# Order of VectorE's work at the end of the head and in the first group of a Strassen-like matmul with RMS norm

## The chip, the cores and the metric

The kernel runs on one core of one Trainium2 chip. The metric is the time of one execution on the device in microseconds (us), lower is better. The time before is the median of three runs.

## The reference

```python
def reference(a, b, gamma, eps):            # all 2048 x 2048, fp32
    x = np.matmul(a, b)
    rms = np.sqrt(np.mean(x ** 2, axis=-1, keepdims=True) + eps)
    return (gamma * x / rms).astype(np.float32)
```

A row of the output needs the whole row of the product (for the root mean square of its 2048 values) before it can be scaled.

## The kernel before

**Tiling.** A is cut into 16 row blocks of 128 rows. B lies in SBUF as bf16, in two halves of 1024 columns (half 0 and half 1), each as two chunks of 512. The first four blocks (0 to 3, `HB = 4`) are the *head*: they are computed while B still arrives. Blocks 4 to 15 follow in six *groups* of two blocks, numbered 2 to 7 (`G0 = 2`), and each group in two halves.

**A group's half** (`group_half`, L576) computes a 256 x 1024 piece of the output by a scheme of Strassen's kind: seven *products* of eight matmuls of 128x512 in place of eight products. Product 1 uses the sum of two quarters of A, product 2 another, and so on; the sums of A (`a_sums`, L254, recorded as L260) are made by VectorE into the five tiles `s_1, s_2, s_5, s_6, s_7`, the sums of B lie ready. The order on TensorE is 2, 5, 1, 4, 3, 7, 6 (5 before 2 in the very first half). Products 4 and 3 add onto the banks of products 2 and 5 (`start=False`), so those banks must have been read before: by ScalarE's copy at L591 and by VectorE's addition at L595. The other evictions are L599 (VectorE, product 1), L602 (ScalarE, product 4's bank), L604 (VectorE, SBUF alone), L607 (ScalarE, product 3's bank), L609 (VectorE, SBUF alone), L613 and L618 (VectorE, products 7 and 6). PSUM has seven banks in the pool `acc` and one more, `tbank`; a new product takes the bank that has been free longest.

**The head's end.** The right half of blocks 2 and 3 (`r2`, `r3`; the code calls them rows) is also made by the seven products; their banks are `pair[2], pair[5], pair[1], p7, p6`. The additions that end these rows stand in three places: the subtraction that reads `pair[1]` (L551), `pair_sums` (L561, L562, SBUF alone) and `pair_ends` (L565, L566, which read `p7` and `p6`). Around L551 stand A's sum 5 for group 2, the copies of block 5's transposes (`take_transposed`, L192), the squares of rows 0 and 1 on ScalarE (`square_half`, L310), `take_rms(0)` (a reduce on VectorE, L335, and a square root on ScalarE, L337), and A's sums 2 and 1.

**Next rows.** While a group is computed, the next two blocks of A are prepared: `row_norm` (ScalarE: two squares L219 and a root L222), `row_factor` (VectorE: four one-column operations, L227 to L232, which bring the block into range for fp16), and `row_apply` (ScalarE: one 128x2048 scaling into fp16, L242), after which the SP queue issues a DMA transpose (L195). `finish(row, halves)` scales rows that are complete (VectorE, `scale`, L370) and stores them (SP queue, L376). POOL's queue loads blocks of A (L116, L121); before some of the loads POOL waits by a one-column copy (L127).

**What sets the order.** The order on each engine is the order in which the program text issues instructions (`tc.manual_schedule()`); waits between engines are derived from the tiles. Work from outside a group is put between its products by *hooks*: `hook(n, f, ...)` in `hooks_of` (L628) appends `f` to a list that `group_half` runs at its n-th place (`at_hook(n)`). Hook 0 stands ahead of the first product, hook 1 behind the first and its copy L591, hook 2 behind the second and L595, hook 3 behind product 1 and L599, hook 4 behind L604. `last_squares` issues squares that were left from the half before.

Of the kernel before, what the change touches and what calls it, by code (L numbers as in the profile page):

```python
# [13 lines left out]
ALU = mybir.AluOpType  # L14
# [3 lines left out]
def kernel(  # L18
# [13 lines left out]
    nc = tc.nc  # L32
# [12 lines left out]
    G0 = HB // 2  # L45
# [148 lines left out]
    def transpose_dma(mb):  # L194
        nc.sync.dma_start_transpose(at(mb), a16[mb])  # L195
# [40 lines left out]
    def row_apply(mb):  # L236
        a16[mb] = a16_slot(mb)
        if mb < HB + 2:

            nc.vector.tensor_scalar_mul(out=a16[mb], in0=a32.pop(mb), scalar1=factor.pop(mb))  # L240
        else:
            nc.scalar.activation(out=a16[mb], in_=a32.pop(mb), func=ACTF.Copy,  # L242
                                 scale=factor.pop(mb))


    def quarter(g, r, c):
        if g < G0:
            return head_at[:, c::2, 2 * g + r, :]
        return at(2 * g + r)[:, c::2, :]

    def sum_of(g, s):
        return s_sum[s].bitcast(BF16) if g < G0 else s_sum[s]

    def a_sums(g, which, lo=0, hi=KP):  # L254
        a11, a12, a21, a22 = (quarter(g, r, c) for r in range(2) for c in range(2))
        terms = {1: (a11, a22, ALU.add), 2: (a21, a22, ALU.add), 5: (a11, a12, ALU.add),
                 6: (a21, a11, ALU.subtract), 7: (a12, a22, ALU.subtract)}
        for s in which:
            x, y, op = terms[s]
            nc.vector.tensor_tensor(out=sum_of(g, s)[:, lo:hi, :], in0=x[:, lo:hi, :],  # L260
                                    in1=y[:, lo:hi, :], op=op)
# [44 lines left out]
    def square_half(mb, h):  # L306
        c = n_sq[mb]
        n_sq[mb] += 1
        sq = sq_pool.tile([P, 2 * CH], BF16, name="sq")
        nc.scalar.activation(out=sq, in_=x_tile(mb, h), func=ACTF.Square,  # L310
                             scale=inv_sqrt_n, accum_out=msq[mb][:, c:c + 1])

    def x_tile(mb, h):


        if (mb, h) not in x_half:
            n = n_x[0]
            n_x[0] += 1
            if n < 8:
                slot = n  # L320
            else:
                g = n // 4
                slot = ((0, 4, 1, 5), (0, 1, 4, 5))[g // 2 % 2 == 0][n % 4] + 2 * (g % 2)
            x_half[mb, h] = x_slot[slot]
        return x_half[mb, h]

    def x_chunk(mb, c):
        return x_tile(mb, c // 2)[:, (c % 2) * CH:(c % 2 + 1) * CH]
# [3 lines left out]
    def take_rms(mb):  # L332

        tot = stat_pool.tile([P, 1], FP32, name="tot")
        nc.vector.reduce_sum(out=tot, in_=msq.pop(mb), axis=mybir.AxisListType.X)  # L335
        rms_of[mb] = stat_pool.tile([P, 1], FP32, name="rms")
        nc.scalar.activation(out=rms_of[mb], in_=tot, func=ACTF.Sqrt)  # L337
# [123 lines left out]
    pair = {}  # L461
# [57 lines left out]
    x11, x12, x21, x22 = (x_chunk(r, c) for r in (r2, r3) for c in (2, 3))  # L519
# [28 lines left out]
    p6 = new_bank()  # L548
    product(PAIR, 1, 6, p6)
    a_sums(G0, (5,))  # L550
    nc.vector.tensor_tensor(out=x22, in0=pair[1], in1=x22, op=ALU.subtract)  # L551
    for g in range(2):
        turn(HB + 1, g)
        take_transposed(HB + 1, g, turned[HB + 1, g], nc.vector.tensor_copy)
    square_half(0, 1)
    square_half(1, 1)
    take_rms(0)
    a_sums(G0, (2, 1))

    def pair_sums():  # L560
        nc.vector.tensor_tensor(out=x11, in0=x22, in1=x21, op=ALU.add)  # L561
# [66 lines left out]
    def hooks_of(g, j):  # L628


        hooks = {n: [] for n in range(8)}
        nxt = 2 * g + 2

        def hook(n, work, *args):
            hooks[n].append(lambda: work(*args))

        def apply(mb):
            row_apply(mb)
            transpose_dma(mb)

        more = g + 1 < NG
        if j == 0:
            if g == G0:
                hook(0, finish, 0, (1,))
                hook(1, row_norm, nxt)
                hook(1, take_rms, 1)
                hook(2, row_factor, nxt)
                hook(2, finish, 0, (0,))
                hook(2, apply, nxt)
                hook(2, row_norm, nxt + 1)  # L650
                hook(2, a_sums, g, (7, 6))
                hook(2, finish, 1, (1, 0))
                hook(2, row_factor, nxt + 1)
                hook(2, pair_sums)
                hook(2, pair_ends)
                hook(4, apply, nxt + 1)
                hook(7, square_half, r2, 1)
            else:
                done = [2 * g - 2, 2 * g - 1]
                if g == G0 + 1:  # L660
                    done.insert(0, r3)
                else:
                    hook(1, row_norm, nxt)
                for mb in done:
                    hook(1, take_rms, mb)
                hook(2, row_factor, nxt)
                hook(2, apply, nxt)
                if g == G0 + 1:
                    hook(2, finish, r3)
                hook(2, row_norm, nxt + 1)  # L670
                hook(3, scale, 2 * g - 2)
                hook(3, row_factor, nxt + 1)
                hook(4, apply, nxt + 1)
                hook(4, store, 2 * g - 2)
        else:
            if g == G0:
                hook(1, take_rms, r2)
                hook(1, square_half, r3, 1)
                hook(2, finish, r2, (1, 0))
            else:  # L680
                hook(2, finish, 2 * g - 1)
            if more:
                hook(3, a_sums, g + 1, (2, 5, 1))
                hook(6, a_sums, g + 1, (7,))
                hook(7, a_sums, g + 1, (6,))
            if g + 2 < NG:
                hook(0, load_after, g, nxt + 2)
                if g == G0:
                    hook(2, wait_for, x_slot[HB + r2][:, 0:1])
                    hook(2, load_block, nxt + 3)  # L690
                    hook(5, row_norm, nxt + 2)
                else:
                    hook(0, load_block, nxt + 3)
        return hooks
# [113 lines left out]
    for g in range(G0, NG - 1):  # L808
        for j in range(2):
            group_half(g, j, hooks_of(g, j))  # L810
# [35 lines left out]
```

## Time and profile before

| what | us |
|---|---|
| median of three runs | 221.8 (221.38 to 221.89) |
| the profiled execution's own time | 221.69 |
| its span, first to last instruction | 219.9 |
| TensorE busy | 209.3 (95%) |
| VectorE busy | 165.9 (75%) |
| ScalarE busy | 127.0 (58%) |
| mean granted TensorE clock | 0.992 |

The span is 1.8 us shorter than the execution's own time. PE is TensorE's matmuls, PEld its weight loads, DVE VectorE, ACT ScalarE, POOL GpSimd, and SP the sync engine, which here only issues DMAs. In the chain of work that ended last, matmuls of L285 (all products) hold 64% of the span: from 69.3 us on they stand one behind the other to the end. The head takes the 69 us ahead of that, bound at first by the arrival of A and B. In the lines shown below a tile's name has its number left out, so that `x`, `s` and `acc` each stand for several buffers, and a line of the code can be that of a helper.

### The profile page before, as it was taken

The page shows a single profiled execution, that of the slowest core. Times are in us where ns is not written, and L with a number is a line of the kernel's source. Part 1 is how long each engine was busy: PE and PEld are TensorE (multiplying, and loading weights), DVE is VectorE, ACT ScalarE, POOL GpSimd, SP SyncE. Part 2 cuts the span into 40 slices and gives each one's busy share as a digit, 9 for nine tenths or more (in the row PEclk, how much of TensorE's full clock was granted, in tenths as well). Part 3 has the DMA queues.
Part 4 walks back from the last instruction along what each step waited for, and adds up shares of the span by engine and source line. Part 5 has one row for each costly group of instructions (what it writes and reads, how often), then busy time and mean ns, then how long its engine had stood idle before and what let it go on. Part 6 is the DMA issues. An engine that isn't in the chain of part 4 may idle for free.

```text
span 219.9 us, 3044 instructions
## 1 busy us (share of the span) xinstructions
PE 209.3 (95%) x1032; PEld 97.4 (44%) x1032; DVE 165.9 (75%) x326; ACT 127.0 (58%) x263; POOL 36.3 (16%) x75
## 2 busy tenths in 40 slices
PE   7799999999999999999999999999999999999970
PEld 3344544444454444444444444444444444444440
DVE  1128799999889999979795639946695659787781
ACT  2110002920599898688745997289747996334471
POOL 7544443343020002100200002000200000000040
PEclk9999999999999999999999999999999999999996
DMA  7999999999929895948799049965699249145045
GB/s 157 164 203 206 199 206 208 212 206 228 409 76 362 291 293 118 358 176 230 213 300 405 3 93 265 351 247 95 156 294 405 42 100 364 73 174 210 1 171 212
DMA packets 36864, 46.60 MB, mean 212 GB/s; under 512 B 22256, under 2 KB 26352, under 8 KB 35568
## 3 DMA queue, kind: packets, MB, share of 16 engines
q0 software_dynamic: 10608, 23.86, 44.1%
q1 hardware_dynamic: 25824, 22.02, 33.5%
q10 hardware_dynamic: 416, 0.52, 0.7%
q8 instruction: 8, 0.13, 0.2%
q14 instruction: 8, 0.07, 0.1%
HBM read 34.60 MB, written 16.78 MB: 234 GB/s over the span
## 4 chain that ended last, share of the span: by engine, by line
PE 65%; DMA 23%; ACT 4%; POOL 2%; issue 1%; DVE 1%; ACTq 0%; POOLq 0%
PE acc L285 64%; DMA b<-in_b_dram 14%; DMA early<-in_a_dram 5%; DMA a<-in_a_dram 4%; ACT sq L219 2%; POOL b L102 1%; ACT at_even L192 1%; PE acc L790 1%; POOL early L106 1%; DVE s L260 1%; DVE at_even L192 0%; ACT x L729 0%; DVE x L551 0%; ACT norm L222 0%; ACT x L531 0%
## 5 line engine op out<-in xcount | busy, mean ns | idle before, releaser
L285 PE MATMUL acc<-b,s 128*128 128x512 bf16 x408 | 93.3, 379 | 0.5 <-DVE s L260 0.5
L285 PEld LDWEIGHTS <-s 128*128 128x128 f16 (+1 forms) x512 | 49.9, 98 | 60.4 <-DVE s L260 1.0
L388 PE MATMUL acc<-b,head_at 128*128 128x512 bf16 x176 | 43.2, 379 | 1.2 <-DMA b<-in_b_dram 1.2
L303 ACT ACTIVATE sq<-x 128x512 bf16<-128x512 f32 x53 | 33.4, 630 | 6.9 <-DVE x L722 3.0
L370 DVE SCALAR_TENSOR_TENSOR x<-x,r,gamma_sb 128x1024 f32<-128x1024 f32 x28 | 34.8, 1282 | 0.7
L219 ACT ACTIVATE sq<-a 128x1024 bf16<-128x1024 f32 x24 | 25.3, 1053 | 2.1 <-DMA a<-in_a_dram 1.5
L388 PEld LDWEIGHTS <-head_at 128*128 128x128 bf16 x176 | 16.9, 98 | 20.6 <-issue 1.6
L242 ACT ACTIVATE head_at<-a,s 128x2048 f16<-128x2048 f32 x10 | 20.0, 1998 | 3.3 <-DVE s L229 3.3
L102 POOL DMA_DIRECT2D b<-in_b_dram x32 | 17.2, 540 | 20.8 <-DMA b<-in_b_dram 15.0
L430 ACT COPY x<-acc 128x512 f32<-128x512 f32 x5 | 2.9, 582 | 24.7 <-PE acc L388 24.7
L285 PEld LDWEIGHTS <-head_at 128*128 128x128 f16 (+1 forms) x112 | 10.9, 98 | 13.2
L285 PE MATMUL acc<-early,head_at 128*128 128x512 bf16 x64 | 14.5, 379 | 0.0
L285 PEld LDWEIGHTS <-at_even 128*128 128x128 f16 x96 | 9.4, 98 | 11.3
L285 PE MATMUL acc<-early,s 128*128 128x512 bf16 x56 | 14.2, 379 | 0.0
L260 DVE TENSOR_TENSOR s<-head_at 128x1024 f16<-128x1024 f16 (+5 forms) x22 | 13.4, 635 | 0.1
L609 DVE TENSOR_TENSOR x<-x,x 128x512 f32<-128x512 f32 x9 | 6.2, 692 | 8.8 <-ACT x L607 8.3
L127 POOL COPY pace<-x 128x1 f32<-128x1 f32 x4 | 1.7, 413 | 66.7 <-DVE x L618 65.6
L591 ACT COPY x<-acc 128x512 f32<-128x512 f32 x9 | 5.2, 573 | 11.5 <-PE acc L285 11.5
L173 DVE COPY head_at<-tbank 128x1024 bf16<-128x1024 bf16 x7 | 4.8, 692 | 8.7 <-PE tbank L168 8.5
L285 PE MATMUL acc<-t_left,s 128*128 128x512 bf16 x48 | 11.3, 379 | 0.0
L774 POOL TENSOR_SCALAR x<-x,r 128x512 f32<-128x512 f32 x1 | 2.7, 2652 | 51.2 <-DVE r L346 51.2
L276 DVE TENSOR_TENSOR b<-b 128x1024 bf16<-128x1024 bf16 x16 | 10.8, 684 | 0.2
(113 smaller groups left out, 237.5 us busy)
## 6 DMA issues: line engine op xcount, KB each, us to landing
out_dram<-x SPq DMA_DIRECT2D x29, 512.0 KB, 3.8
a<-in_a_dram POOLq DMA_DIRECT2D x10, 1024.0 KB, 8.7
b<-in_b_dram POOLq DMA_DIRECT2D x32, 256.0 KB, 10.0
a<-in_a_dram POOLq DMA_DIRECT2D x4, 512.0 KB, 9.8
early<-in_a_dram POOLq DMA_DIRECT2D x7, 256.0 KB, 10.2
gamma_sb<-in_gamma_dram POOLq DMA_DIRECT2D x2, 512.0 KB, 8.3
out_dram<-x SPq DMA_DIRECT2D x3, 256.0 KB, 2.6
out_dram<-a SPq DMA_DIRECT2D x1, 512.0 KB, 3.3
```

The lines of the kernel that those rows point to most:

```text
L102: nc.gpsimd.dma_start(out=raw[j][kp][:, t, :], in_=b[lo:lo + P, j * HALF:(j + 1) * HALF])
L173: nc.vector.tensor_copy(out=head_at[:, 2 * kp:2 * kp + 2, :, :], in_=view)
L219: nc.scalar.activation(out=junk, in_=a32[mb][:, h * HALF:(h + 1) * HALF], func=ACTF.Square, scale=2.0 ** -8, accum_out=n2[:, h:h + 1])
L242: nc.scalar.activation(out=a16[mb], in_=a32.pop(mb), func=ACTF.Copy, scale=factor.pop(mb))
L260: nc.vector.tensor_tensor(out=sum_of(g, s)[:, lo:hi, :], in0=x[:, lo:hi, :], in1=y[:, lo:hi, :], op=op)
L276: nc.vector.tensor_tensor(out=flat[:, 1:3, :], in0=flat[:, 1:3, :], in1=flat[:, 0::3, :], op=ALU.add)
L285: nc.tensor.matmul(bank, lhsT[:, kp, :], rhs, start=(start and kp == 0), stop=(kp == KP - 1), skip_group_check=not start)
L303: nc.scalar.activation(out=sq[:, 0:CH], in_=src, func=ACTF.Square, scale=inv_sqrt_n, accum_out=msq[mb][:, c:c + 1])
L370: nc.vector.scalar_tensor_tensor(out=x, in0=x, scalar=inverse_of[mb], in1=gamma_sb[:, h * HALF:(h + 1) * HALF], op0=ALU.mult, op1=ALU.mult)
L388: nc.tensor.matmul(bank, head_at[:, kt, r, :], head_rhs(c, kt), start=(kt == 0), stop=(kt == KT - 1))
L591: nc.scalar.copy(out=c, in_=one[1])
L609: nc.vector.tensor_tensor(out=t, in0=t, in1=x12, op=ALU.add)
```

## The change

At the head's end A's sums 2 and 1 for group 2 go ahead of `take_rms(0)`, and the subtraction L551 moves from ahead of the two copies of transposes to behind these sums (and ahead of `take_rms(0)`). In the first half of group 2, in hook 2, `pair_sums`, `pair_ends` and A's sums 7 and 6 go to the front of the list: ahead of the first `row_factor`, of the scalings of rows 0 and 1 and of the second `row_factor`. No instruction is added or taken out.

```diff
     a_sums(G0, (5,))
-    nc.vector.tensor_tensor(out=x22, in0=pair[1], in1=x22, op=ALU.subtract)
     for g in range(2):
         turn(HB + 1, g)
         take_transposed(HB + 1, g, turned[HB + 1, g], nc.vector.tensor_copy)
     square_half(0, 1)
     square_half(1, 1)
+    a_sums(G0, (2, 1))
+    nc.vector.tensor_tensor(out=x22, in0=pair[1], in1=x22, op=ALU.subtract)
     take_rms(0)
-    a_sums(G0, (2, 1))
...
                 hook(0, finish, 0, (1,))
                 hook(1, row_norm, nxt)
                 hook(1, take_rms, 1)
+                hook(2, pair_sums)
+                hook(2, pair_ends)
+                hook(2, a_sums, g, (7, 6))
                 hook(2, row_factor, nxt)
                 hook(2, finish, 0, (0,))
                 hook(2, apply, nxt)
                 hook(2, row_norm, nxt + 1)
-                hook(2, a_sums, g, (7, 6))
                 hook(2, finish, 1, (1, 0))
                 hook(2, row_factor, nxt + 1)
-                hook(2, pair_sums)
-                hook(2, pair_ends)
                 hook(4, apply, nxt + 1)
                 hook(7, square_half, r2, 1)
```

In the two built programs the order of instructions changes on VectorE alone; TensorE, ScalarE, POOL and SP have theirs unchanged. Because banks come free in another order, some products sit in other banks: product 7 and 6 of group 2's half 0 take those of block 5's transposes and of `pair[1]`, and in half 1 products 2 and 5 take the banks of `p7` and `p6`, and product 1 the one that L602 reads.

## The prediction, made before the changed kernel was run

> **What bounds the kernel now.** I read the page first, then TensorE's waits, then the timelines of TensorE, VectorE and ScalarE (columns: start us, length us, engine, line, operation, tiles, count, idle before and its releaser) between 66 and 88 us, where the moved instructions stand.
>
> ```profile
> PE 209.3 (95%) x1032; PEld 97.4 (44%) x1032; DVE 165.9 (75%) x326; ACT 127.0 (58%) x263; POOL 36.3 (16%) x75
> ```
>
> ```profile
> PE acc L147 <- DVE pace L137: 1.4, 1, 1.4
> ...
> PE acc L285 <- DVE s L260: 0.5, 1, 0.5
> ```
>
> TensorE is busy for 95% of the span. In the stretch that the change touches it waits once, for A's sums (L260). All else must show as a TensorE wait or it costs nothing.
>
> ```profile
> 66.97 1.89 PE L285 MATMUL acc<-b,s 128*128 128x512 bf16 x8
> 69.32 1.90 PE L285 MATMUL acc<-b,s 128*128 128x512 bf16 x8 [0.46 <-DVE s L260]
> 71.06 1.89 PE L285 MATMUL acc<-t_left,s 128*128 128x512 bf16 x8
> 72.78 3.62 PE L285 MATMUL acc<-t_left,at_even 128*128 128x512 bf16 x16
> 83.14 1.89 PE L285 MATMUL acc<-early,s 128*128 128x512 bf16 x8
> 84.87 3.62 PE L285 MATMUL acc<-early,at_even 128*128 128x512 bf16 x16
> ```
>
> These are, for group 2 (rows 4 and 5): products 5, 2, 1, then 4 and 3 of half 0; then 1, and 4 and 3, of half 1 (7, 6 and the next 2, 5 lie between). A product takes 1.725 us from start to start (72.78 less 71.06), one matmul 0.216.
>
> ```profile
> 66.66 0.68 DVE L551 TENSOR_TENSOR x<-acc,x 128x512 f32<-128x512 f32 x1
> 68.57 1.29 DVE L260 TENSOR_TENSOR s<-at_even 128x1024 f16<-128x1024 f16 x2
> 71.33 0.69 DVE L595 TENSOR_TENSOR t_first<-acc,head_at 128x512 f32<-128x512 f32 x1
> 72.07 0.15 DVE L227 TENSOR_SCALAR s<-norm 128x1 f32<-128x1 f32 x1
> 78.46 0.68 DVE L561 TENSOR_TENSOR x<-x 128x512 f32<-128x512 f32 x1
> 79.17 0.69 DVE L562 TENSOR_TENSOR x<-x,x 128x512 f32<-128x512 f32 x1
> ```
>
> VectorE has hardly a gap here. Its steps from start to start: 0.60 for a 128x512 or 128x1024 operation, 0.71 where it waits for the result just before it (L561 to L562), 0.70 for the four small row factors, 1.20 for a scaling (L370).
>
> ```profile
> 72.64 2.00 ACT L242 ACTIVATE head_at<-a,s 128x2048 f16<-128x2048 f32 x1 [0.52 <-DVE s L229]
> 77.10 0.57 ACT L602 COPY x<-acc 128x512 f32<-128x512 f32 x1
> 78.33 2.00 ACT L242 ACTIVATE head_at<-a,s 128x2048 f16<-128x2048 f32 x1
> 82.64 0.57 ACT L591 COPY x<-acc 128x512 f32<-128x512 f32 x1
> ```
>
> The reader is to see that ScalarE starts L242 as soon as VectorE's row factor (L229) is there, and then works 10.00 us without a gap until L591 of half 1. That copy ends at 83.21; product 4 of half 1, which adds into the bank that L591 reads, starts at 84.87. The slack is 1.66 us.
>
> **What the Trainium skill says.** PSUM — Partial Sum Buffer, section "Engine vs sequencer instructions": the queues of ScalarE and VectorE are "strict FIFO". The trace agrees: L602's product ended at about 74.7 (72.78 + 1.73 + 0.16), yet it ran at 77.10, behind a normalization that it has nothing to do with. TensorE: Matmul & The Clock Gate, section "Why this matters for your kernels", warns of TensorE gaps over about 3 us, which halve its clock. In this trace the clock is 1.00 for the 3.4 us after the last matmul and 0.51 after that.
>
> **The change, part by part.**
>
> *Head: sums ahead of the subtraction.* VectorE does L260 (sum 5) at 66.05 in both. Then, in place of L551, comes the first L192 copy. It needs the transposes that end at 66.68, so 66.72; the second 67.32; sum 2, which waits for it, 67.32 + 0.71 = 68.03, to 68.72. TensorE was let go 0.06 after the sum before (69.26 to 69.32), so product 2 starts at 68.78; its own order allows 68.48 + 0.22 = 68.70. Gain at this point 0.54. Sum 1 runs at 68.63, its product at 70.51: no wait.
>
> *What the subtraction and take_rms pay.* Subtraction at 69.23, reduce (L335) 69.83 to 69.97 in place of 68.46. Behind that reduce stands ScalarE: the square root (L337) starts 0.04 later, 70.01 to 70.21, and L591 (half 0), queued behind it, ends at 70.74 and not 69.48. VectorE's reciprocal waits for the root: 70.25; scaling 70.44; the next reduce 71.64; L595 at 71.80 to 72.49, against 72.02 before. Product 4 of half 0 adds into the bank that L595 reads: allowed at 70.51 + 1.73 = 72.24, released at 72.49 + 0.06 = 72.55. So 0.31 of the 0.54 is given back; it starts 0.23 ahead of before (72.78).
>
> *First group: six operations ahead of the row factor.* After L595: L561 72.40, L562 73.11, L565 73.72, L566 74.32, sums 7 and 6 at 74.93 and 75.53 (the second ends at 76.21), then L227 at 76.13. Products 7 and 6 start at 76.00 and 77.73 and need the sums by then: done at 75.61 and 76.21, cover 0.39 and 1.5. The banks of pair products 7 and 6 come free near 74.4 and 75.0, some 6 us sooner than before; no matmul waited for them, so nothing is gained.
>
> The factor (L229) is ready at 76.13 + 0.38 + 0.15 = 76.66, and L242 starts at 76.70: 4.06 us later than before (the six operations 3.73, L595's lateness 0.47, less 0.14 for which L227 waited before). ScalarE has idled for it since 73.5. All that is queued behind it moves by as much: the second norm, L602 (ends 81.73), the second L242 (82.39), L607 (ends 84.86), a square, L591 of half 1: 86.70 to 87.27. The second row factor is no tighter: its norm ends at 81.25, VectorE has finished the scalings of rows 0 and 1 by 80.7, the factor is there at 81.8.
>
> TensorE: product 4 of half 0 at 72.55, then 3, 7, 6, 2, 5, 1 at steps of 1.725; product 4 of half 1 could go at 72.55 + 7 x 1.725 = 84.63. It is released at 87.27 + 0.06 = 87.33: a stall of 2.70. Product 1 of half 1 takes the bank that L602 frees (81.73 against 82.90), cover 1.2. Against before: 87.33 - 84.87 = **+2.46 us**, since every later product of before is back to back.
>
> *Moved DMAs.* Of the moved scalings and applies, SP's queue issues, in order: store of x_4 (+0.5), of x_0 (+4.1), the first transpose (near 78.7, its issue takes 3.2), stores of x_5 and x_1 (82.0), the second transpose (84.4, landing 4.6 later, 89.0). L591 of half 1 writes x_5, so it also needs that store landed: 82.0 + 2.9 (as before) = 84.9, against 86.70; the window's slowest store took 6.6, which would give 88.6, 1.9 more stall. POOL waits for the second transpose, so the load of block 8 moves from 85.53 to 89.6 and lands 5.6 later, as before; ScalarE's norm of it and L591 of group 3 follow at 97.9 to 98.4. Group 3's product 2 starts at 84.87 + 6.9 + 2.46 = 94.23, its product 4 needs that copy at 99.41: cover 0.9, used if the load takes over 6.5. Its half 1 is closer: L591 ends at 107.20 + 4.06 = 111.26, product 4 is due at 109.04 + 2.46 = 111.50: cover 0.2. Later ScalarE gaps of 2.1 and 3.8 us, where it waits for TensorE, absorb the rest.
>
> Sum: profiled span 219.9, with 1.8 around it 221.69; 221.69 + 2.46 = 224.15. The median shown is 221.8, 0.1 over that run: **224.2**.
>
> **Unknown costs.** TensorE's release by L595 and L591 isn't seen as a wait in this stretch; I take 0.06 (from L260), bounds 0.0 and 0.2. VectorE's first copy may wait on transposes up to 0.2 longer or not at all: -0.1 to +0.2, since it shifts the whole chain. The store of x_5: nothing to +1.9. Group 3's covers: nothing to +0.8. None can bring a gain beyond 0.2, as each is a wait.
>
> **Rivals.** *Cover holds (not slower).* The end depends on one place, product 4 of half 1. If ScalarE were ready for L591 there by 84.63 - 0.06 - 0.57 = 84.0, so that L242 began by 74.0 (a delay under 1.4 us, not 4.06), nothing would stall and the head's gain stays: 221.69 - 0.23 = 221.5; 221.15 if L595 doesn't stall either. For it: before has 1.66 us of slack, and the change removes the one wait named. Against: ten microseconds of ScalarE work without a gap, in order.
>
> *More behind it.* The same stall, and a second: TensorE is idle from 84.80 (last matmul's end) to 87.33, 2.5 us; a store or load that lands late can stretch it past the 3.4 us at which this trace's clock fell. A restart at 0.51 for about as long (3.4 us) costs 1.7: 225.9. A late x_5 store gives up to 226.1, group 3's covers up to 225.0. Against: 2.5 is under 3.4.
>
> *Less.* VectorE's order is what is built, so the row factor can't come before 75.9; only short waits differ: 223.3.
>
> **How the numbers follow.** Forecast (223.6 to 224.9) 0.64; more behind it (225 to 227) 0.18; less (222.7 to 223.5) 0.06; cover holds (220.9 to 221.6) 0.12. The range 222.9 to 225.9 leaves out the cover case and a few hundredths of the long ones. A measurement of this kernel can tell about 0.3% (0.7 us) from no change: faster (under 221.1) 0.03, same 0.09, slower 0.88.
>
> **What would show it.** Right: L242's idle before the first apply near 3 us behind L229; in TensorE's waits a new line of about 2.7 us, released by ScalarE's L591, near 84.6; one of 0.3 behind L595; L260's 0.5 shrunk to 0.1. Wrong: no TensorE gap near 84 to 88; L242 starting before 74; a gap much over 2.7, or a second one near 99 or 111, or a clock under 1.00 after it.

## The result, and the profile after

The changed kernel takes 227.4 us (median of five, 226.9 to 228.1), 1.025 times the kernel before (95% interval 1.021 to 1.030), whose median in five executions was 221.6; a second set of the changed kernel (227.0, `f0_after_again`, below) gave 1.024 (1.021 to 1.027). It was forecast slower, at 224.2 in a range of 222.9 to 225.9. The direction held, the size did not: about +5.5 us against the +2.4 forecast. The profiled execution took 227.87, with a span of 226.1.

TensorE's waits (the engine and line waited for, then us in total, times, longest), and its timeline from group 2 on:

```profile
PE acc L285 <- ACT x L591: 2.5, 1, 2.5
...
PE acc L285 <- DVE s L227: 0.3, 1, 0.3
```

```profile
73.19 3.61 PE L285 MATMUL acc<-t_left,at_even 128*128 128x512 bf16 x16
...
87.95 5.30 PE L285 MATMUL acc<-early,at_even 128*128 128x512 bf16 x16 [2.52 <-ACT x L591]
...
101.92 1.89 PE L285 MATMUL acc<-t_left,head_at 128*128 128x512 bf16 x8
104.10 1.89 PE L285 MATMUL acc<-t_left,head_at 128*128 128x512 bf16 x8 [0.30 <-DVE s L227]
...
114.76 3.61 PE L285 MATMUL acc<-early,head_at 128*128 128x512 bf16 x15
```

The wait for A's sums (L260) is gone and the forecast stall behind L591 is there (87.95). But the two products that follow it last 5.30 us in place of 3.62, and three more waits stand in group 3, at 101.92, 104.10 and 114.76. (Two of them show only in the start: 1.73 us is a product's step, and these stand 1.93 and 2.03 behind the start before them. For the one at 104.10 the profile names L227; L595, one instruction ahead of it on VectorE and the reader of that bank, ended at 104.05.)

ScalarE, POOL, VectorE and SP in the same stretch:

```profile
70.75 0.20 ACT L337 ACTIVATE rms<-tot 128x1 f32<-128x1 f32 x1 [1.26 <-DVE tot L335]
...
77.34 2.00 ACT L242 ACTIVATE head_at<-a,s 128x2048 f16<-128x2048 f32 x1 [3.27 <-DVE s L229]
...
87.33 0.57 ACT L591 COPY x<-acc 128x512 f32<-128x512 f32 x1
...
98.74 1.06 ACT L219 ACTIVATE sq<-a 128x1024 bf16<-128x1024 f32 x1 [4.11 <-DMA a<-in_a_dram]
...
101.30 0.57 ACT L591 COPY x<-acc 128x512 f32<-128x512 f32 x1
...
114.15 0.57 ACT L591 COPY x<-acc 128x512 f32<-128x512 f32 x1
```

```profile
89.75 1.18 POOL L127 CAST pace<-head_at 128x1 f32<-128x1 f16 x1 [22.68 <-DMA head_at<-head_at]
90.88 0.53 POOL L121 DMA_DIRECT2D a<-in_a_dram  x1
```

```profile
89.60 2.48 DVE L370 SCALAR_TENSOR_TENSOR x<-x,r,gamma_sb 128x1024 f32<-128x1024 f32 x2
90.91 1.53 SPq L376 DMA_DIRECT2D out_dram<-x  x2
```

Before, the same two POOL lines, the stores of row 2 on SP's queue, and the later places that hang on the load read:

```profile
85.02 0.18 POOL L127 CAST pace<-head_at 128x1 f32<-128x1 f16 x1 [18.71 <-DMA head_at<-head_at]
85.53 0.53 POOL L121 DMA_DIRECT2D a<-in_a_dram  x1 [0.32 <-ACT rms L337]
87.05 1.53 SPq L376 DMA_DIRECT2D out_dram<-x  x2
91.24 1.06 ACT L219 ACTIVATE sq<-a 128x1024 bf16<-128x1024 f32 x1 [1.37 <-DMA a<-in_a_dram]
106.64 0.56 ACT L591 COPY x<-acc 128x512 f32<-128x512 f32 x1
109.04 3.62 PE L285 MATMUL acc<-early,head_at 128*128 128x512 bf16 x16
```

The new line to read is L219 at 98.74: ScalarE stands 4.11 us for block 8 of A, then runs to L591 of group 3's half 0 and on to that of half 1, and TensorE waits for both.

The head's end differs by more than 1 us from one profiled execution to the next, of one kernel too. So I count from the first matmul of group 2's product 5 (66.97 before, 67.68 after, 66.54 in the changed kernel's second trace, called "again"):

| start, from product 5's (us) | before | after | again |
|---|---|---|---|
| group 2, half 0, product 4 | 5.81 | -0.30 | -0.30 |
| group 2, half 1, product 4 | 17.90 | +2.37 | +2.36 |
| group 2, half 1, product 7 | 21.35 | +4.06 | +2.36 |
| group 3, half 0, product 4 | 29.99 | +4.25 | +4.32 |
| group 3, half 0, product 3 | 31.72 | +4.70 | +4.77 |
| group 3, half 1, product 4 | 42.07 | +5.01 | +5.06 |
| group 4, half 0, product 1 | 52.43 | +5.01 | +5.06 |

Behind the last row nothing more is lost up to the last product: L790 stands +5.00 in "after". What whole executions show beyond these 5 us lies ahead of product 5 or behind the last matmul.

The two traces of one kernel differ in the middle and agree at the end. In "after" the granted clock fell behind the stall (columns: window; length; busy of PE, PEld, DVE, ACT, POOL; clock, DMA share, GB/s), in "again" it did not:

```profile
88.00:93.00 5.00, 5.00 (x16) 1.94 (x16) 4.19 (x6) 3.74 (x10) 2.85 (x4) 0.66 0.52 133
```

```profile
87.00:92.00 5.00, 5.00 (x25) 2.27 (x24) 4.19 (x6) 4.69 (x13) 2.88 (x4) 1.00 0.51 132
```

The whole executions agree. Of the eleven of the changed kernel, the seven with a mean clock of 0.981 to 0.984 took 227.2 us on average, the three with 0.992 to 0.995 took 227.0 (the eleventh, at 0.988, took 228.1). In "again" the 1.7 us that the clock left alone were waited for in group 3:

```profile
86.80 3.61 PE L285 MATMUL acc<-early,at_even 128*128 128x512 bf16 x16 [2.50 <-ACT x L591]
...
100.85 1.89 PE L285 MATMUL acc<-t_left,head_at 128*128 128x512 bf16 x8 [1.80 <-ACT x L591]
```

So something other than the stall sets the end. The theory: the late work of group 2 delays the load of block 8 (issued 4.6 later than before, landed 6.8 later, both from product 5), and group 3, with 1.78 us to spare for it (in before, product 4 of half 1 starts at 109.04, L591 ends at 107.20, and a release takes 0.06), waits for the rest: 6.80 - 1.78 = 5.02 us, which is what the table shows. Stall and clock lie beneath that wait. The rivals: the stall and the clock's drop simply add up; or other things that moved (banks, the subtraction) cost the time.

### The profile page after: what moved, and what is told of

Its sections match the earlier page's. It is cut to its first block, busy times and chain, and to the rows that moved or that the text cites. A ratio compares the mean times of both kernels' runs of the same rounds, so it can differ in the third digit from the quotient of the medians.

```text
span 226.1 us, 3023 instructions
## 1 busy us (share of the span) xinstructions
PE 211.4 (94%) x1012; PEld 98.4 (44%) x1032; DVE 166.1 (73%) x326; ACT 127.0 (56%) x263; POOL 37.0 (16%) x75
## 4 chain that ended last, share of the span: by engine, by line
PE 50%; DMA 29%; issue 13%; ACT 4%; DVE 1%; POOL 1%; POOLq 0%; ACTq 0%
PE acc L285 49%; DMA b<-in_b_dram 16%; DMA a<-in_a_dram 8%; DMA early<-in_a_dram 4%; ACT sq L219 2%; PE acc L790 1%; ACT sq L303 1%; DVE gamma_sb L240 1%; POOL pace L127 0%; POOL a L121 0%; ACT x L591 0%; ACT x L729 0%; DVE x L595 0%; ACT x L607 0%; POOL gamma_sb L511 0%
## 5 line engine op out<-in xcount | busy, mean ns | idle before, releaser
L388 PE MATMUL acc<-b,head_at 128*128 128x512 bf16 x171 | 42.0, 379 | 1.4 <-DMA b<-in_b_dram 1.3
L370 DVE SCALAR_TENSOR_TENSOR x<-x,r,gamma_sb 128x1024 f32<-128x1024 f32 x28 | 34.8, 1281 | 0.7
L219 ACT ACTIVATE sq<-a 128x1024 bf16<-128x1024 f32 x24 | 25.3, 1054 | 5.0 <-DMA a<-in_a_dram 4.4
L242 ACT ACTIVATE head_at<-a,s 128x2048 f16<-128x2048 f32 x10 | 20.0, 1997 | 6.1 <-DVE s L229 6.1
L285 PE MATMUL acc<-early,at_even 128*128 128x512 bf16 x47 | 12.5, 422 | 2.6 <-ACT x L591 2.5
L260 DVE TENSOR_TENSOR s<-head_at 128x1024 f16<-128x1024 f16 (+5 forms) x22 | 13.4, 635 | 0.1
L127 POOL COPY pace<-x 128x1 f32<-128x1 f32 x4 | 1.3, 320 | 67.4 <-DVE x L618 67.4
L591 ACT COPY x<-acc 128x512 f32<-128x512 f32 x9 | 5.2, 573 | 11.5 <-PE acc L285 7.7
L285 PE MATMUL acc<-t_left,head_at 128*128 128x512 bf16 x48 | 11.0, 379 | 0.3 <-DVE s L227 0.3
```

Of the source, the lines that this page charges most:

```text
L219: nc.scalar.activation(out=junk, in_=a32[mb][:, h * HALF:(h + 1) * HALF], func=ACTF.Square, scale=2.0 ** -8, accum_out=n2[:, h:h + 1])
L285: nc.tensor.matmul(bank, lhsT[:, kp, :], rhs, start=(start and kp == 0), stop=(kp == KP - 1), skip_group_check=not start)
L370: nc.vector.scalar_tensor_tensor(out=x, in0=x, scalar=inverse_of[mb], in1=gamma_sb[:, h * HALF:(h + 1) * HALF], op0=ALU.mult, op1=ALU.mult)
L388: nc.tensor.matmul(bank, head_at[:, kt, r, :], head_rhs(c, kt), start=(kt == 0), stop=(kt == KT - 1))
L591: nc.scalar.copy(out=c, in_=one[1])
```

## The experiments

**The head alone.** `e1_head_only` is the kernel before with the head's half of the diff.

```diff
     a_sums(G0, (5,))
-    nc.vector.tensor_tensor(out=x22, in0=pair[1], in1=x22, op=ALU.subtract)
...
+    a_sums(G0, (2, 1))
+    nc.vector.tensor_tensor(out=x22, in0=pair[1], in1=x22, op=ALU.subtract)
     take_rms(0)
-    a_sums(G0, (2, 1))
```

> Only the head's part of the change. VectorE's row factor comes 0.5 us later than before, so ScalarE's first apply L242 is late by 0.5, inside the 1.66 us of slack ahead of group 2's product 4 of half 1. All theories in which the late row factor is the cause: 0.2 to 0.5 us faster than before (0.54 won at product 2, about 0.3 given back behind L595), 221.0 to 221.4. Rival 'other banks or the subtraction's place is the cause': slower by 1 us or more.

Measured: 222.1 us, 1.0027 (1.0018 to 1.0036): slower, not faster. In its trace the head gain is there (product 4 of half 0 starts 0.31 sooner, from product 5), and it is lost again, with 0.34 more, at one place:

```profile
81.52 1.89 PE L285 MATMUL acc<-b,s 128*128 128x512 bf16 x8 [0.46 <-DVE x L565]
```

Product 5 of half 1 takes the bank of pair product 7, and L565, still at its old place in the queue and now 1.2 us later from product 5 (80.78 less 66.73, against 79.78 less 66.97), frees it too late. In the full change L565 comes early, and its trace has no such wait. So the head's half with its banks costs 0.3%, and the rival's "1 us or more" fails.

**The hooks alone.** `e2_hooks_only` is the changed kernel with the head's half undone.

> Only the first group's part. L242 is late by 3.6 us. 'Stall alone' (the forecast's step): L591 of half 1 lets product 4 go at 86.86 instead of 84.87, +2.0, 223.5; with a clock drop on top ('stall plus clock') +3.7, 225.2. 'Late load' (the late transpose delays the load of block 8 by 3.6 and POOL's wait and the landing add about 2.7; group 3 has 1.8 us of slack for it): +4.6, 226.2, with a TensorE gap at group 3's product 4 of half 1 behind ScalarE's L591.

Measured: 226.3 us, 1.0225 (1.020 to 1.025), 4.8 us more than before by the medians: the "late load" figure, and too much for the stall with or without the clock. The trace shows both waits:

```profile
86.93 3.61 PE L285 MATMUL acc<-early,at_even 128*128 128x512 bf16 x16 [1.79 <-ACT x L591]
...
101.14 5.30 PE L285 MATMUL acc<-t_left,head_at 128*128 128x512 bf16 x16 [1.96 <-ACT x L591]
```

Block 8 landed 30.85 us from product 5, 6.7 later than before. In this execution, which took 227.7, the clock fell behind the second wait, where nothing later hides it; in the other four (226.0 to 226.6) the mean clock was 0.989 or more.

**Row factors ahead.** `e3_factors_first` is the changed kernel with this hook 2:

```diff
+                hook(2, row_factor, nxt)
                 hook(2, pair_sums)
                 hook(2, pair_ends)
                 hook(2, a_sums, g, (7, 6))
-                hook(2, row_factor, nxt)
                 hook(2, finish, 0, (0,))
                 hook(2, apply, nxt)
                 hook(2, row_norm, nxt + 1)
+                hook(2, row_factor, nxt + 1)
                 hook(2, finish, 1, (1, 0))
-                hook(2, row_factor, nxt + 1)
```

> The whole change, but both row factors go ahead: the first to the front of hook 2, the second ahead of the scaling of row 1. The six moved VectorE operations stay ahead of the scalings and the banks come free as in the changed kernel. If the late row factor is the cause of everything: L242 is late by 0.5 only, no ScalarE stall, no drop of the clock, no late load; product 7 may wait some 0.3 for sum 7; 221.3 to 221.9. Rival 'the moved operations or the other banks are the cause': 225 or more.

Measured: 228.1 us, 1.031 (1.028 to 1.035): my expectation was wrong by 6 us. L242 was 1.2 us later than before, and not 4.0, counted from product 5; yet:

```profile
77.20 7.08 PE L285 MATMUL acc<-b,s 128*128 128x512 bf16 x32 [1.18 <-DVE s L260]
...
101.75 6.54 PE L285 MATMUL acc<-t_left,head_at 128*128 128x512 bf16 x16 [3.05 <-ACT x L591]
```

The first wait: the row factor stood 0.88 for its norm in VectorE's queue, and sum 7 behind it. The last is the load of block 8 again, landed 7.4 later than before, though the apply was early: the second transpose landed 5.0 later, and the load took 2.3 longer. SP's queue tells why the transposes were late:

```profile
71.72 7.65 SPq L376 DMA_DIRECT2D out_dram<-x  x2
79.46 3.30 SPq L195 DMA_TRANSPOSE head_at<-head_at  x1
```

The first transpose was ready at 75.8 (end of L242) and issued at 79.46, behind the store of row 0's left half, whose scaling still stood behind the moved operations. So the late row factor alone is not the cause: with it mended, the other moved work still makes the load late.

**The transpose ahead of the store.** `g1_transpose_first` is e3 with one hook moved.

```diff
+                hook(2, apply, nxt)
                 hook(2, finish, 0, (0,))
-                hook(2, apply, nxt)
```

> e3 with one more hook moved: the apply and transpose of block 6 are issued ahead of the store of row 0's left half, so that on SP's queue the first transpose no longer stands behind a store whose scaling is late (in e3 it was ready at 75.8 and issued at 79.5). Theory 'SP's order carries the lateness to the load of block 8': the second transpose lands about 2 us earlier, the load too, group 3's wait of 3.1 shrinks below 1 and the time falls to 223 to 225. 'Only the place of VectorE's operations matters': 228, as e3.

Measured: 225.4 us, 1.0152 (1.0124 to 1.018). The first transpose was issued at 75.82, the second landed 2.0 us sooner than in e3, and the load of block 8 1.5 sooner. VectorE's operations stand as in e3, so SP's order does carry lateness to the load. But group 3's wait shrank only to 2.14, where I had expected less than 1: the load, issued 2.2 sooner than in e3, took 8.6 us to land (7.9 in e3). And of the 2.7 us by which the time fell, the load explains 1.5. The rest fits the clock, which fell behind e3's wait of 3.05 and in five of g1's six executions stayed (a mean of 0.989 or more; the ratio is theirs). In the sixth it was 0.976, and the time 229.7.

**Twelve matmuls in the gap.** `f1_busy` and `f5_busy_clean` are the changed kernel with unread matmuls ahead of group 2's product 4 of half 1:

```diff
         at_hook(3)
+        if (g, j) == (G0, 1):
+            junk = ps_t.tile([P, CH], FP32, name="tbank")
+            for _ in range(12):
+                nc.tensor.matmul(junk, identity, b_quarter(1, 0, 0, 0), start=True, stop=True)
         product(g, j, 4, p2, start=False)
```

> The changed kernel with twelve matmuls more, which nobody reads, into the free bank tbank ahead of group 2's product 4 of half 1: 12 x 0.216 = 2.6 us, as long as TensorE stands there for ScalarE's L591. The clock has no idle time to fall in. 'Stall plus clock': the 1.7 us that products 4 and 3 lost go away, 225.7. 'Late load': block 8 lands as late as before, group 3 waits for it all the same, and the time that the clock gives back is waited there: 227.4.

> f1 mended: the twelve unread matmuls use the identity and a part of B, which nobody writes any more, so that they wait for nothing. TensorE has no idle time at group 2's product 4, the clock stays. 'Late load sets the end': 227.2, as the changed kernel. 'Stall plus clock': 225.6.

f1 used `sum_of(g, 1)[:, 0, :]` in place of the identity, a sum that hook 3 had just ordered to be made anew for group 3. So TensorE waited 9.1 us for it, and f1 (235.5 us, 1.063) says nothing on the question; nor does `f3_both` (below; 237.5, 1.071), where it waited 10.4. f5: 227.3 us, 1.0258 (1.022 to 1.029), no different from the changed kernel's 227.0 in its second set. There was no idle time at group 2 and no drop of the clock, and group 3 waited instead:

```profile
84.61 2.75 PE L604 MATMUL tbank<-b,identity 128*128 128x512 bf16 x12
87.29 3.61 PE L285 MATMUL acc<-early,at_even 128*128 128x512 bf16 x16
...
101.13 1.89 PE L285 MATMUL acc<-t_left,head_at 128*128 128x512 bf16 x8 [1.60 <-ACT x L591]
```

**The load earlier.** `f2_early_load` issues the load of block 8 as soon as its buffer is free; `f4_load_behind_l618` moves POOL's wait to the result of L618:

```diff
-        wait_for(at(2 * g + 3)[:, KT - 1, 0:1] if g == G0 else x_chunk(2 * g + 1, 1)[:, 0:1])
+        wait_for(x_chunk(2 * g + 1, 1)[:, 0:1])
```

> The changed kernel with the load of block 8 issued without the wait for the second transpose, so as soon as its buffer is free (near 79 instead of 91 us). 'Late load': group 3's waits (0.2, 0.45 and 0.3 us in the changed kernel's trace) go, the stall at group 2 and the clock's drop stay: 226.4; where the clock does not drop, 224.7. 'Stall plus clock' with the load harmless: 227.4.

> The changed kernel with POOL's wait ahead of the load of block 8 put on the result of L618 (near 86.6 us) in place of the second transpose's landing (89.7), so that the load starts near 87, after the store of x_5 has landed, and not near 90.5. 'Late load': group 3's waits go. What stays is the stall of 2.7 less the 0.3 won in the head, 223.9, and 1.7 more, 225.6, where the clock falls in the stall. 'Load harmless': 227.2.

f2: 227.0 us, 1.0235 (1.021 to 1.026). Group 3's waits went, but the load, issued at 78.86, ran beside the first transpose and the store of x_5. That store landed 5.5 us after its issue (2.9 before), and L591 stood for it: a stall of 3.99 in place of 2.5, and the clock fell.

```profile
88.01 0.59 ACT L591 COPY x<-acc 128x512 f32<-128x512 f32 x1 [1.37 <-DMA out_dram<-x]
```

f4: 226.2 us, 1.0187 (1.016 to 1.022). Load issued at 87.88, POOL's wait 0.18, landed after 5.2: no wait in group 3. In five of its six executions the mean clock was 0.983 to 0.986 and the time 225.8 to 226.7; in one it was 0.992 and the time 224.5. Here the clock's drop is no longer hidden and costs some 1.8 us. The one execution at 224.5, which has no trace, fits the forecast's stall with nothing else.

**Both.** `f6_both_clean` is f4 with f5's matmuls (`f3_both` was f2 with f1's).

> Both at once: twelve unread matmuls in the gap, and the early load. 'Late load' and 'clock' as two covers of each other: both must be taken away to get what the forecast counted, 221.55 + 2.7 - 0.3 = 223.9 to 224.7. If either alone were the cause, one of the two kernels before would already be here.

> f4 and f5 together. Late load and clock both taken away: what the forecast had counted, 223.9 to 224.3.

Measured f6: 224.6 us, 1.0125 (1.011 to 1.014), +2.8 us; in its trace every product from product 4 of group 2's half 1 on stands +2.36, with no wait. (The twelve matmuls fill the stall and don't replace it: L591 ends at 88.20, 0.05 ahead of product 4.)

```profile
88.25 3.61 PE L285 MATMUL acc<-early,at_even 128*128 128x512 bf16 x16
...
100.34 3.62 PE L285 MATMUL acc<-t_left,head_at 128*128 128x512 bf16 x16
```

Four kernels, two causes that cover each other: neither removed 227.0 (the repeat `f0_after_again`), clock alone 227.3, load alone 226.2, both 224.6. Only with both gone is the forecast's stall what remains.

> The changed kernel once more, on the chip of the next three, to compare with. All theories: 227.4 (226.9 to 228.1).

**The reduce between the sums.** `e4_rms_between` has before's first group and, in the head, sum 2, then `take_rms(0)`, then sum 1 and the subtraction.

```diff
+    a_sums(G0, (2,))
     take_rms(0)
-    a_sums(G0, (2, 1))
+    a_sums(G0, (1,))
+    nc.vector.tensor_tensor(out=x22, in0=pair[1], in1=x22, op=ALU.subtract)
```

> Before's first group, and the head with sum 2 first, then take_rms(0), then sum 1 and the subtraction. If L595 is late in the changed head because the reduce stands behind sum 1 and the subtraction, then here product 2 starts 0.5 earlier than before and product 4 has no wait: 0.5 us faster than before, 221.0. If L595 is late for another reason: as e1, 221.3.

Measured: 221.2 us, 0.9981 (0.9969 to 0.9993): faster than before by 0.2%, against the 0.5 us expected. From product 5 all later products stand 0.52 us ahead of before, without a wait; in whole executions 0.3 to 0.4 us of it is seen. So L595 was late in the changed head because the reduce stood behind sum 1 and the subtraction.

## Why the prediction was right or wrong

*Right, with their sizes.* Product 2 no longer waits; product 4 of half 0 comes 0.30 sooner (0.23 forecast), held by L595 behind the late reduce and root, whose wait the trace shows (L337's 1.26). L242 idles 3.27 behind L229 ("near 3"). L591 of half 1 releases product 4 at +2.37 (+2.46 forecast), a stall of 2.68 counted from where its own order had put it (2.70 forecast). f6 shows that this chain by itself gives 224.6, and the one execution of f4 in which the clock stayed took as long (224.5) without the extra matmuls.

*Wrong: the step that failed.* "The load of block 8 moves from 85.53 to 89.6 and lands 5.6 later, as before", with covers in group 3 of 0.9 and 0.2, and "nothing to +0.8" kept for them in the range. The mechanism was named, and its term mis-sized: group 3 added 2.65 us to the stall's 2.37. The second transpose landed +4.02 from product 5, as forecast. Then two durations that I had carried over from before did not hold:

- From that landing to the load's issue: 1.18 us in place of 0.56. POOL's one-column copy (L127) itself took 1.18 and not 0.18, as it now fell beside VectorE's scaling of row 2 (L370, the first of the two 89.60 to 90.88). SBUF — State Buffer of the Trainium skill, section "Who interferes with whom", says that a VectorE instruction with two SBUF inputs contends with a GpSimd instruction that reads SBUF; L370 has two, `x` and `gamma_sb`. The traces agree: in before, the copy beside the end of an addition with one input in PSUM took 0.18, and the next one, beside an L370, 1.10. In "after", "again", e2, e3, f5 and g1 the copy ahead of this load took 0.37 to 1.22 us and ended within 0.06 of the end of an L370, however early it had begun.
- From issue to landing: 7.78 in place of 5.62. Before, the load had a lead of 1.5 us over the store of row 2 and 2.7 over the load of block 9; now the store follows within 0.03 and the other load after 1.2. With before's leads or longer (e1, e4, f4, f6) it took 5.2 to 6.1; with the store within 0.05 or ahead of it (again, e2, e3, f5, g1) 7.7 to 8.6. VectorE's scaling beside the load's issue is no rival, since before had it too (85.73). That the others' traffic is the cause fits these traces but was not tried by itself, and no run moved the store and the second load far enough apart to tell which of them counts.

Together the landing was late by 6.80 and not 4.06, and from it to group 3's product 4 of half 1 TensorE's release takes the same 16.1 us as before. The slack there was 1.78, which the forecast had seen (109.04 less 107.20, less the release): the end moves by 5.02 and not by the stall's 2.4. The prediction's own signs of being wrong came true here: second waits in group 3, at 101.92 and 114.76, and a clock under 1.00.

*Half right: "More behind it".* The clock did fall after an idle time of 2.5 us, which I had thought too short, and cost 1.7 as priced. But 227.4 lies above that rival's range too (225 to 227), which gave each second cause a price by itself. In the changed kernel the clock's loss is spent where TensorE would have waited for block 8 anyway, so that it costs nothing (f5), and with the load mended it costs 1.8 (f4). The forecast allowed 0.8 us for a longer landing of the load, and did not ask what would run beside it.

*Also missed.* The late scalings work through SP's queue as the late factor does through ScalarE's: e3 had the factor 2.8 us sooner than the changed kernel and was no faster.

## What to carry to other kernels

When a reordering makes an engine late, follow every DMA that it issues to the next wait on its data, and look again at what will run beside the transfer then; its old duration may not hold (here 7.8 us in place of 5.6). Stalls in a row need not add: the end is set by the latest release, and an earlier loss (here a fallen clock) fills waiting time that would have been there; take causes away in pairs before calling one harmless. A queue's order (SP's stores ahead of transposes) is part of the dependency chain even where the engines' waits look right.

## What the runs showed of the hardware that was not expected

The granted clock is not told by the length of TensorE's gap: it fell behind gaps of 1.96 us (e2), 2.52 (after), 2.51 (f4), 3.05 (e3) and 3.99 (f2), and stayed behind gaps of 1.79 (e2), 2.14 (g1) and 2.50 (again). A drop stretched the sixteen matmuls behind it from 3.6 to 5.2 to 6.5 us. TensorE: Matmul & The Clock Gate of the Trainium skill, section "Why this matters for your kernels", puts the bound at about 3 us; these runs show drops below it.
